# Where layer 0's sixth modulation vector is summed: inside the attention, or beside the attention's output projection

## The chip, the cores and the metric

The program runs on one core of a Trainium2 chip. The metric is the device time of one execution in microseconds. Five engines work side by side, each through its own list of instructions in a fixed order: TensorE (PE; its weight loads are PEld), VectorE (DVE), ScalarE (ACT), GpSimd (POOL) and SyncE (SP, which here issues the DMA transfers). An instruction that must wait for another engine or for a transfer holds up everything behind it on its own engine.

## The reference

A trunk of two layers over a sequence of 1024 rows of width 1024, all in float32. Layer 0 mixes by an attention with forget gates (16 heads of 64), layer 1 by gated linear attention (GLA), and each is followed by a SwiGLU channel mixer (FFN). Before and after each of these stand factors that are computed from one conditioning vector c:

```python
c_act = jax.nn.silu(c)
for i in range(DEPTH):
    mod = c_act @ ada_w[i] + ada_b[i]
    sh1, sc1, g1, sh2, sc2, g2 = jnp.split(mod, N_MOD, axis=-1)
    h = modulate(rms_norm(x, norm1_g[i]), sh1, sc1)
    ...
    x = x + g1[:, None, :] * y
    h = modulate(rms_norm(x, norm2_g[i]), sh2, sc2)
    x = x + g2[:, None, :] * swiglu(h, ffn_w_in[i], ffn_w_out[i])
```

So `mod` has six parts of 1024 numbers per layer, each a vector of 1024 times a matrix of 1024 x 1024. The kernel calls them j = 0 to 5. Layer 0's parts 0 and 1 are needed at the start, part 2 (the gate of the attention) from its output projection on, parts 3 and 4 when the channel mixer's input is made, and part 5 (the gate of the channel mixer) only where the channel mixer's output is added to x.

## The kernel before

Every large product is done as three products of rounded halves (`mm3`, L286 to L288: high by high, low by high, high by low), so each float32 operand is split into a high part (ScalarE, a cast) and a low part (VectorE or GpSimd, a subtraction). The attention of layer 0 goes over eight pairs of heads p = 0 to 7. While pair p's scores (L1132 to L1135), softmax (L1138 to L1144, VectorE, ScalarE and GpSimd), transposes (`t_b`, L1164) and outputs (L1176, L1178) are done, the projections of pair p + 1 are woven in between them on TensorE (`qk_proj`, `v_half`). The last pair, attention(7), is woven together with `fox_tail`: the output projection over the first four of eight blocks of the inner dimension (`out_chunk(0, 4, ...)`, tiles fo000 to fo071: block row m, half of the sequence). After it, `last_chunk(4, 4, ...)` does the other four blocks (tiles fo0400 and up for the first half, fo1401 and up for the second). Each group of products ends with a VectorE instruction that multiplies by the gate g1 and adds into x (L1277; in the changed file L1279). Sums of squares (`ss`, L718 and L725) for the next normalisation follow in `last_chunk`.

The modulation vectors are summed on VectorE by the generator `ada_steps(l, j, acc, raw_of, nt, ahead)`. One step loads nt x 128 rows of ada_w's part j by four DMAs (L423, each into 32 partitions) into a raw tile, and then does nt multiply-adds of 128 x 256 into the accumulator `acc` (L442 for the first of a vector, L444 for the others; c's numbers are the scalars). With nt = 4 a vector has 8 steps, with nt = 2 it has 16; either way it has 32 multiply-adds. At its end two small products with `four` (L449) add up the quarters, and VectorE adds ada_b (L452).

When a step is emitted is set by the class `Pace`: a call `ada0(t)` adds t to a balance, and steps are run as long as the balance is not negative, each taking off what it yields (1.0 for a step with ahead = 0). Before the change four vectors, j = 2 to 5, stand in the queue `ada0` as 8 steps and one end each, 36 units; `qk_proj` adds 3.3 at its end for p = 2 to 7, twice each, 12 times. Their raw tiles come from the ring `wr` of three slots, which the weight loads (L209) use as well. The accumulator `acc0` uses a quarter of a slot of its own, [128, 2, 512] float32: its first half's first 256 columns. Layer 1's vectors stand in a second queue, `ada1`, with nt = 2 and tiles named ad_s.

The emitted order is not yet the order on the engines. A scheduler with a timeline of its own orders each engine's instructions; `tc.issue_after(x)` adds the condition that an instruction comes behind x, and `last_of("D")` is the last instruction emitted for VectorE so far.

Of the kernel before, what the change touches and what calls it, by code (L numbers as in the profile page):

```python
# [9 lines left out]
F32 = mybir.dt.float32  # L10
# [6 lines left out]
P = 128  # L17
# [3 lines left out]
HALF = 512  # L21
# [32 lines left out]
def trunk(ctx, tc, x, c, ada_w, ada_b, norm1_g, norm2_g, ffn_w_in, ffn_w_out,  # L54
# [253 lines left out]
    acc_r = Ring(big, acc_sl)  # L308
# [65 lines left out]
    for t in range(6):  # L374
        nt, src = (4, rows2[0:8, :]) if t < 4 else (2, crow)
# [35 lines left out]
    def ada_steps(l, j, acc, raw_of, nt, ahead):  # L411


        steps, got = deque(range(32 // nt)), deque()

        def load():
            if not steps:
                return
            n = steps.popleft()
            raw = raw_of([P, nt * 256], F32, f"ada{l}{j}{n}").rearrange("p (t c) -> p t c", t=nt)  # L420
            src = ada_w[l, 32 * nt * n:32 * nt * (n + 1), j * D:(j + 1) * D]
            for q in range(4):
                nc.sync.dma_start(raw[32 * q:32 * q + 32],  # L423
                                  src[:, 256 * q:256 * q + 256].rearrange("(r t) c -> r t c", t=nt))
            got.append(raw)

        for _ in range(ahead):
            load()
        for n in range(32 // nt):
            load()  # L430
            if ahead:
                yield ADA_A
            raw = got.popleft()
            with ExitStack() as es:
                if ahead:
                    es.enter_context(tc.issue_after(last_of("D")))
                elif n == 0:
                    es.enter_context(tc.issue_after(split_after["D"]))
                for t in range(nt):
                    o = (0 if nt == 4 else 32) + t * (32 // nt) + n  # L440
                    if n == t == 0:
                        nc.vector.tensor_scalar(acc, raw[:, t], c42[:, o:o + 1], None, op0=ALU.mult)  # L442
                    else:
                        nc.vector.scalar_tensor_tensor(acc, raw[:, t], c42[:, o:o + 1], acc,  # L444
                                                       op0=ALU.mult, op1=ALU.add)
            yield ADA_B if ahead else 1.0
        mp = pj([P, 2, 4], F32, f"mp{l}{j}")
        for b in range(2):
            nc.tensor.matmul(mp[:, b], acc[:, psl(b)], four, start=True, stop=True)  # L449
        o = l * 48 + j * 8  # L450
        qb = lambda t: t.rearrange("p (q b) -> p b q", b=2)
        nc.vector.tensor_add(qb(modc[:, l, j]), mp, qb(vec[:, o:o + 8]))  # L452
        for i, jj in ((0, 1), (1, 4)):
            if j == jj:
                make_a(l, i)
        yield 1.0
# [23 lines left out]
    ada0, ada1 = Pace(), Pace()  # L480
# [616 lines left out]
    def qk_proj(p, i):  # L1097

        if i == 0:
            qkt[p] = qk_tiles(p)  # L1100
        wt = feed.next()
        feed.depth = 3
        for hf in range(2):
            ps = pj([P, HALF], F32, f"qk{i}{p}{hf}")
            yield from proj(ps, wt, hT, hf)
            (k_evac if i else q_evac)(ps, qkt[p], hf)
        if p > 1:
            ada0(3.3)

    oTs = {}  # L1110

# [95 lines left out]
    def attention(p):  # L1207
        for a in range(2):
            for g in ORDER:
                u = (p, a, g)  # L1210
                lps = yield from scores(u)
                if pending[0] is not None:
                    yield from finish(*pending[0])
                pending[0] = (u, lps)
        if p == 7:
            yield from finish(*pending[0])
# [2 lines left out]
        for g in gs:  # L1219
            yield from g  # L1220

    acc0 = acc_r([P, 2, HALF], F32, "acc0")[:, 0, 0:256]
    for j in (2, 3, 4, 5):
        ada0.q.append(ada_steps(0, j, acc0, wr, 4, 0))
    run(v_half(0, 0, gates_end))
    q_evac(accs[1][1][1], qkt[0], 1)
# [76 lines left out]
    oh = new_h("oh")  # L1303
    x_slots = idle + [list(otr.q)[-1]]
    xs = [big.tile([P, S], F32, tag=x_slots[k], name=f"x0_{k}") for k in range(8)]

    def fox_tail():
        for k in range(4):
            reload_h(oT_d, oh, k, "or")

        nc.sync.dma_start(xs[0], xT_d[0])

        def ahead(k):
            if 3 <= k < 6:
                reload_h(oT_d, oh, k + 1, "or")
            if k < 7:
                nc.sync.dma_start(xs[k + 1], xT_d[k + 1])
            yield 0.01

        yield from out_chunk(0, 4, oh, xs, 0, 2, "fo", (0, 1), before=ahead)  # L1320

    weave(attention(7), 27.0, fox_tail(), 36.0, LAGS)
    split(oh[7].hi, oh[7].lo, oTs[7])
    dump_d("oT", oT_d)
# [17 lines left out]
    def ffn(l, oh, xs, slots, nm, mid, norm_end, each=None):  # L1342
# [13 lines left out]
        pj, psr = ps_rings(6, 2)  # L1356
# [7 lines left out]
        sv = Views(slots["to"], 2, [HALF], f"ss{l}").v  # L1364
# [30 lines left out]
                split_t((b["B11"] + b["B21"])[k], ya[k], sh(k))  # L1395
            return gates

        last_chunk(4, 4, oh, xs, l, 2, nm, sv, norm, psr=psr)
        dump(f"xa{l}", xs)
        sg = opr_["sg"]  # L1400
        rb = rms_rows(ss1[0], f"{l}11", psr)
# [336 lines left out]
        sv = Views(slots["b"][0:4], 2, [HALF], f"se{l}").v  # L1738
# [27 lines left out]
    ADA_A, ADA_B = 6.0, 3.0  # L1766
# [25 lines left out]
    ADA_A, ADA_B = 2.6, 1.0  # L1792
# [260 lines left out]
    oh = new_h("gh")  # L2053
# [8 lines left out]
    xs = [big.tile([P, S], F32, tag=x_slots[k], name=f"x1_{k}") for k in range(8)]  # L2062
# [39 lines left out]
    ADA_A, ADA_B = 12.0, 6.0  # L2102
# [31 lines left out]
```

## Time and profile before

| | |
|---|---|
| median of 3 runs | 2396.82 us (2395.17 to 2397.31) |
| profiled execution | 2397.77 us |
| its span in the trace | 2396.1 us |
| granted TensorE clock | 0.997 |
| TensorE busy | 2368.3 us (99%) |
| VectorE busy | 1776.6 us (74%) |
| multiply-adds of layer 0's j = 2 to 5 | 142 to 474 us |
| first and last residual add of `fox_tail` | 522 and 601 us |
| residual adds of `last_chunk`, first half | 617 to 628 us |

The span is what the profiler saw from first to last instruction; the profiled execution's own time is 1.7 us longer. In the rows that are quoted below a line such as "L444 DVE" is the source line and the engine, an arrow leads from inputs to the output, and x is a count. A row of waits says which engine, at which line, waited for what: us in all, times, longest. A row of the chain has its start, its length and what it was. A row of the timeline has the start, the length, the instruction and, in brackets, how long the engine stood idle before it and what ended that.

### The profile page before, as it was taken

What the parts mean: (1) busy time and instruction counts of PE and PEld (TensorE: products, weight loads), DVE (VectorE), ACT (ScalarE), POOL (GpSimd) and SP (SyncE); (2) the same over time, 40 slices, a digit from 0 to 9 for tenths busy, and PEclk for the clock granted to TensorE, in tenths of its full rate; (3) what the DMA queues carried; (4) which work ended last, traced back from release to release, by engine and by line L of the source; (5) the groups of instructions that cost most, each with busy time, mean ns of one, the idle gap of its engine ahead of it and who ended that gap; (6) DMA issues with size and microseconds to landing.
All of it is one profiled execution on the core that took longest, in us unless ns stands there. A gap on an engine that the chain in (4) does not pass through costs nothing.

```text
span 2396.1 us, 35784 instructions
## 1 busy us (share of the span) xinstructions
PE 2368.3 (99%) x12344; PEld 2016.8 (84%) x12344; DVE 1776.6 (74%) x3016; ACT 1127.8 (47%) x2164; POOL 1008.5 (42%) x911
## 2 busy tenths in 40 slices
PE   8999999999999999999999999999999999999998
PEld 7888888888888888888888888898888888888888
DVE  6577878886698788876798666655687877775787
ACT  6666555674443333345325645353343333345326
POOL 1333333333445666643264321222345666643262
PEclk9999999999999999999999999999999999999999
DMA  7422424342435544557655242334424544457664
GB/s 254 145 89 90 131 84 128 106 138 83 150 109 173 179 166 165 171 196 261 229 187 162 67 119 80 107 112 135 136 96 161 183 145 159 154 182 256 228 202 146
DMA packets 335773, 363.42 MB, mean 152 GB/s; under 512 B 24348, under 2 KB 277432, under 8 KB 335592
## 3 DMA queue, kind: packets, MB, share of 16 engines
q1 hardware_dynamic: 335592, 361.15, 45.9%
q8 instruction: 97, 1.59, 0.3%
q14 instruction: 84, 0.69, 0.1%
HBM read 268.19 MB, written 92.86 MB: 151 GB/s over the span
## 4 chain that ended last, share of the span: by engine, by line
PE 90%; DVE 5%; DMA 2%; ACT 1%; issue 1%; POOL 0%; SPq 0%; DVEq 0%; POOLq 0%; ACTq 0%
PE p_b L288 16%; PE p_b L286 16%; PE p_b L287 16%; PE t_b L1164 2%; PE o_b L1178 2%; PE qk_b L286 2%; PE qk_b L287 2%; PE qk_b L288 2%; PE vps_b L286 1%; PE vps_b L288 1%; PE vps_b L287 1%; PE s_b L1132 1%; PE s_b L1133 1%; PE gr_b L286 1%; PE gr_b L287 1%
## 5 line engine op out<-in xcount | busy, mean ns | idle before, releaser
L175 DVE TENSOR_TENSOR o_s<-xv_s,o_s 128x512 fp32r<-128x512 f32 (+1 forms) x376 | 324.1, 867 | 66.1 <-ACT o_s L174 65.6
L174 ACT CAST o_s<-xv_s 128x512 fp32r<-128x512 f32 (+1 forms) x376 | 216.2, 587 | 303.6 <-PE p_b L288 248.0
L287 PE MATMUL p_b<-B,o_s 128*128 128x512 f32 x608 | 237.8, 391 | 0.0
L288 PE MATMUL p_b<-B,o_s 128*128 128x512 f32 x608 | 237.5, 391 | 0.0
L286 PE MATMUL p_b<-B,o_s 128*128 128x512 f32 x608 | 236.3, 392 | 0.0
L1144 POOL TENSOR_SCALAR lp_s<-lp_s,st 128x128 f32<-128x128 f32 (+7 forms) x128 | 99.0, 778 | 291.1 <-DVE st L1143 280.7
L843 POOL TENSOR_TENSOR ex_s<-xv_s,xv_s 128x512 f32<-128x512 f32 (+1 forms) x64 | 85.5, 1335 | 292.8 <-DMA xv_s<-in_ffn_w_in_dram 120.7
L286 PE MATMUL p_b<-T,o_s 128*128 128x512 f32 x480 | 186.7, 389 | 0.0
L287 PE MATMUL p_b<-T,o_s 128*128 128x512 f32 x480 | 186.7, 389 | 0.0
L288 PE MATMUL p_b<-T,o_s 128*128 128x512 f32 x480 | 181.2, 389 | 0.0
L287 PEld LDWEIGHTS p_b<-B,o_s 128*128 128x128 f32 x608 | 115.0, 189 | 23.9
L286 PEld LDWEIGHTS p_b<-B,o_s 128*128 128x128 f32 x608 | 115.0, 189 | 23.8
L288 PEld LDWEIGHTS p_b<-B,o_s 128*128 128x128 f32 x608 | 114.7, 189 | 24.0
L1142 ACT ACTIVATE lp_s<-lp_s,st 128x128 f32<-128x128 f32 (+7 forms) x128 | 99.3, 777 | 65.2 <-DVE st L1138 62.1
L174 ACT CAST pt_s<-t_b 128x512 fp32r<-128x512 f32 (+1 forms) x160 | 79.7, 547 | 75.4 <-PE t_b L1164 73.9
L845 POOL TENSOR_TENSOR xv_s<-ex_s,xv_s 128x512 f32<-128x512 f32 (+1 forms) x64 | 88.1, 1377 | 60.7 <-DVE o_s L175 58.2
L1521 DVE TENSOR_TENSOR ex_s<-ex_s,p_b 128x512 f32<-128x512 f32 x140 | 93.7, 681 | 23.4 <-PE p_b L288 23.2
L227 POOL TENSOR_TENSOR w_l_s<-w__s,w_h_s 128x256 fp32r<-128x256 f32 x90 | 69.7, 803 | 94.7 <-ACT w_h_s L223 56.7
L175 DVE TENSOR_TENSOR pt_s<-t_b,pt_s 128x512 fp32r<-128x512 f32 (+1 forms) x160 | 96.2, 631 | 15.9 <-ACT pt_s L174 15.3
L287 PEld LDWEIGHTS p_b<-T,o_s 128*128 128x128 f32 x480 | 90.1, 188 | 18.7
L286 PEld LDWEIGHTS p_b<-T,o_s 128*128 128x128 f32 x480 | 90.1, 188 | 18.7
L288 PEld LDWEIGHTS p_b<-T,o_s 128*128 128x128 f32 x480 | 90.1, 188 | 18.6
(1954 smaller groups left out, 7392.9 us busy)
## 6 DMA issues: line engine op xcount, KB each, us to landing
xv_s<-in_ffn_w_in_dram SPq DMA_DIRECT2D x176, 256.0 KB, 3.3
hid_B<-x SPq DMA_DIRECT2D x70, 512.0 KB, 2.6
ad_s<-in_ada_w_dram SPq DMA_DIRECT2D x384, 64.0 KB, 2.4
hid_T<-x SPq DMA_DIRECT2D x36, 512.0 KB, 2.8
xv_s<-in_ffn_w_out_dram SPq DMA_DIRECT2D x96, 192.0 KB, 5.3
ada_s<-in_ada_w_dram SPq DMA_DIRECT2D x128, 128.0 KB, 2.8
xv_s<-in_ffn_w_out_dram SPq DMA_DIRECT2D x40, 256.0 KB, 2.9
T2o<-hid_T SPq DMA_DIRECT2D x18, 512.0 KB, 8.4
```

What stands on the lines that cost most here:

```text
L174: nc.scalar.copy(hi, src)
L175: nc.vector.tensor_sub(lo, src, hi.bitcast(F32))
L227: (nc.gpsimd if i < 3 else nc.vector).tensor_sub(lo[:, cs], rw[:, cs], hi[:, cs].bitcast(F32))
L286: nc.tensor.matmul(ps, ah, bh, start=start, stop=False)
L287: nc.tensor.matmul(ps, ah, bl, start=False, stop=False)
L288: nc.tensor.matmul(ps, al, bh, start=False, stop=stop)
L843: nc.gpsimd.tensor_add(s1, a21, a22)
L845: nc.gpsimd.tensor_sub(a11, s1, a11)
L1142: nc.scalar.activation(lp, lp, AF.Exp, bias=mcur, scale=-1.0, accum_out=st[:, qi, 2:3])
L1144: nc.gpsimd.tensor_scalar(lp, lp, st[:, qi, 3:4], 1.0, op0=ALU.mult, op1=ALU.mult)
L1164: nc.tensor.transpose(tp[:, i, :], lps[qi][:, psl(2 * b + jj)], ident)
L1521: nc.vector.tensor_add(d, d if src is None else dest(G, src), ps)
```

## The change

Vector j = 5 leaves the queue that the attention works off. It is put into `ada0` again just before attention(7) and `fox_tail` are woven, with nt = 2, and its raw tile is the other half of the accumulator's slot (`raw0`), a single one. So each of its 16 steps loads 4 x 64 KB where a step before loaded 4 x 128 KB, and no load can start before the two multiply-adds of the step ahead of it have read `raw0`. The steps are paid by 1.05 after each of the 16 groups of `out_chunk`; a step takes off 0.7 + 0.3. The conditions `if ahead` become `if nt == 2`, so that j = 5 yields between its load and its multiply-adds and has its multiply-adds behind the last emitted VectorE instruction; for layer 1's vectors, all nt = 2, nothing differs. The pace in `qk_proj` goes from 3.3 to 2.4 a call, for 27 units. What might be left is paid in `last_chunk`, and a `flush` stands behind it.

```diff
@@ ada_steps
-            if ahead:
+            if nt == 2:
                 yield ADA_A
             raw = got.popleft()
             with ExitStack() as es:
-                if ahead:
+                if nt == 2:
                     es.enter_context(tc.issue_after(last_of("D")))
...
-            yield ADA_B if ahead else 1.0
+            yield ADA_B if nt == 2 else 1.0
@@ qk_proj
         if p > 1:
-            ada0(3.3)
+            ada0(2.4)
@@ the queue
-    acc0 = acc_r([P, 2, HALF], F32, "acc0")[:, 0, 0:256]
-    for j in (2, 3, 4, 5):
+    acc0 = acc_r([P, 2, HALF], F32, "acc0")
+    raw0 = acc0[:, 1]
+    acc0 = acc0[:, 0, 0:256]
+    for j in (2, 3, 4):
         ada0.q.append(ada_steps(0, j, acc0, wr, 4, 0))
@@ fox_tail
-        yield from out_chunk(0, 4, oh, xs, 0, 2, "fo", (0, 1), before=ahead)
-
+        yield from out_chunk(0, 4, oh, xs, 0, 2, "fo", (0, 1), before=ahead, after=lambda m, hf: ada0(1.05))
+
+    ADA_A, ADA_B = 0.7, 0.3
+    ada0.q.append(ada_steps(0, 5, acc0, Cycle([raw0]), 2, 0))
     weave(attention(7), 27.0, fox_tail(), 36.0, LAGS)
@@ ffn
-        last_chunk(4, 4, oh, xs, l, 2, nm, sv, norm, psr=psr)
+        last_chunk(4, 4, oh, xs, l, 2, nm, sv, norm, psr=psr, meanwhile=lambda: ada0(1.0))
+        ada0.flush()
```

The engines' orders differ from attention(1) up to the start of `last_chunk`; from there to the end of the program they are the same. The numbers in tile names count tiles and differ between the files. At three places:

SyncE's transfers in the second half of the projection (wo: the projection's weights; xv: the channel mixer's). Before:

```order
L209 DMA wo_768_s_78_7081<-in_fox_w_out_dram 128x4x256
L209 DMA wo_512_s_77_7040<-in_fox_w_out_dram 128x4x256
L209 DMA wo_0_s_79_7123<-in_fox_w_out_dram 128x4x256
L209 DMA wo_256_s_80_7164<-in_fox_w_out_dram 128x4x256
L825 DMA xv_s_7330<-in_ffn_w_in_dram 128x4x128 x2
L209 DMA wo_512_s_81_7244<-in_fox_w_out_dram 128x4x256
L209 DMA wo_768_s_82_7285<-in_fox_w_out_dram 128x4x256
```

And now (acc_s is the accumulator's slot, here its half `raw0`; x16 are four steps):

```order
L423 DMA acc_s_1_753<-in_ada_w_dram 32x2x256 x4
L209 DMA wo_768_s_70_7105<-in_fox_w_out_dram 128x4x256
L423 DMA acc_s_1_753<-in_ada_w_dram 32x2x256 x4
L209 DMA wo_512_s_69_7064<-in_fox_w_out_dram 128x4x256
L423 DMA acc_s_1_753<-in_ada_w_dram 32x2x256 x16
L209 DMA wo_0_s_71_7147<-in_fox_w_out_dram 128x4x256
L423 DMA acc_s_1_753<-in_ada_w_dram 32x2x256 x12
L209 DMA wo_256_s_72_7188<-in_fox_w_out_dram 128x4x256
L423 DMA acc_s_1_753<-in_ada_w_dram 32x2x256 x4
L825 DMA xv_s_7354<-in_ffn_w_in_dram 128x4x128 x2
L423 DMA acc_s_1_753<-in_ada_w_dram 32x2x256 x4
L209 DMA wo_512_s_73_7268<-in_fox_w_out_dram 128x4x256
```

The loads of steps 5 to 15 stand among the weight loads, four to sixteen at a time, and the weights and the channel mixer's first loads behind them.

VectorE's instructions from the last groups of `fox_tail` to the first residual add of `last_chunk` (lp, st and pt: softmax and the probabilities' low parts; oT: the attention's output; ohl: its low part). Before:

```order
L1277 SCALAR_TENSOR_TENSOR x_7_6234<-fo070p_b_63_6981,modc,x_7_6234 128x512
L1143 RECIPROCAL st_6858<-st_6858 128x1
L1193 TENSOR_TENSOR oT_s_8_6384<-o_b_63_6905,ot_6940 64x256
L1277 SCALAR_TENSOR_TENSOR x_7_6234<-fo071p_b_64_7006,modc,x_7_6234 128x512
L227 TENSOR_TENSOR wo_512l_s_66_7043<-wo_512_s_77_7040,wo_512h_s_65_7042 128x256
L175 TENSOR_TENSOR pt_s_158_6949<-t_b_158_6944,pt_s_158_6949 128x512
L175 TENSOR_TENSOR pt_s_159_6960<-t_b_159_6955,pt_s_159_6960 128x512
L175 TENSOR_TENSOR pt_s_160_6970<-t_b_160_6966,pt_s_160_6970 128x384
L227 TENSOR_TENSOR wo_256l_s_72_7167<-wo_256_s_80_7164,wo_256h_s_71_7166 128x256
L1193 TENSOR_TENSOR oT_s_8_6384<-o_b_64_6943,ot_6999 64x256
L175 TENSOR_TENSOR ohl_6226<-oT_s_8_6384,ohh_6225 128x1024
L1277 SCALAR_TENSOR_TENSOR x_0_6227<-fo0400p_b_1_7050,modc,x_0_6227 128x512
```

And now:

```order
L227 TENSOR_TENSOR wo_512l_s_66_7067<-wo_512_s_69_7064,wo_512h_s_65_7066 128x256
L1193 TENSOR_TENSOR oT_s_8_6324<-o_b_63_6905,ot_6946 64x256
L175 TENSOR_TENSOR pt_s_158_6955<-t_b_158_6950,pt_s_158_6955 128x512
L175 TENSOR_TENSOR pt_s_159_6966<-t_b_159_6961,pt_s_159_6966 128x512
L175 TENSOR_TENSOR pt_s_160_6976<-t_b_160_6972,pt_s_160_6976 128x384
L444 SCALAR_TENSOR_TENSOR acc_s_1_753<-acc_s_1_753,c_164 128x256 x2
L227 TENSOR_TENSOR wo_256l_s_72_7191<-wo_256_s_72_7188,wo_256h_s_71_7190 128x256
L1193 TENSOR_TENSOR oT_s_8_6324<-o_b_64_6949,ot_7013 64x256
L444 SCALAR_TENSOR_TENSOR acc_s_1_753<-acc_s_1_753,c_164 128x256 x2
L175 TENSOR_TENSOR ohl_6150<-oT_s_8_6324,ohh_6149 128x1024
L444 SCALAR_TENSOR_TENSOR acc_s_1_753<-acc_s_1_753,c_164 128x256 x2
L1279 SCALAR_TENSOR_TENSOR x_0_6151<-fo0400p_b_1_7074,modc,x_0_6151 128x512
```

The multiply-adds of steps 13, 14 and 15 stand between the attention's last instructions, step 15's right ahead of fo0400's residual add (step 12's stand two rows ahead of the first row here).

TensorE at the change from the fifth and sixth block rows of `last_chunk` to the seventh. Before:

```order
L287 MATMUL fo0440p_b_5_7133<-ohl_6226,wo_512h_s_65_7042 128x512
L288 MATMUL fo0440p_b_5_7133<-ohh_6225,wo_512l_s_66_7043 128x512
L287 MATMUL fo0450p_b_6_7148<-ohl_6226,wo_512h_s_65_7042 128x512
L288 MATMUL fo0450p_b_6_7148<-ohh_6225,wo_512l_s_66_7043 128x512
L286 MATMUL fo0460p_b_7_7174<-ohh_6219,wo_768h_s_67_7083 128x512
L287 MATMUL fo0460p_b_7_7174<-ohl_6220,wo_768h_s_67_7083 128x512
```

And now:

```order
L286 MATMUL fo0450p_b_6_7172<-ohh_6149,wo_512h_s_65_7066 128x512
L287 MATMUL fo0450p_b_6_7172<-ohl_6150,wo_512h_s_65_7066 128x512
L288 MATMUL fo0450p_b_6_7172<-ohh_6149,wo_512l_s_66_7067 128x512
L449 MATMUL mp_b_64_7040<-four,acc_s_1_753 128x4 x2
L286 MATMUL fo0460p_b_7_7198<-ohh_6143,wo_768h_s_67_7107 128x512
L287 MATMUL fo0460p_b_7_7198<-ohl_6144,wo_768h_s_67_7107 128x512
```

The two small products of vector 5, which need its finished sum, stand ahead of fo0460 now; the three products of fo0450 above them stood some rows further up before.

## The prediction

> **What bounds the kernel now.** I read the page's engine table first, then its chain, and after that, for the two stretches that the change touches, the windows, the waits and the chain inside them.
>
> ```profile
> span 2396.1 us, 35784 instructions
> PE 2368.3 (99%) x12344; PEld 2016.8 (84%) x12344; DVE 1776.6 (74%) x3016; ACT 1127.8 (47%) x2164; POOL 1008.5 (42%) x911
> PE 90%; DVE 5%; DMA 2%; ACT 1%; issue 1%; POOL 0%; SPq 0%; DVEq 0%; POOLq 0%; ACTq 0%
> ```
>
> TensorE bounds the program: 2368.3 of 2396.1 us busy, 90% of the chain. The change takes no product away, so time can come only out of the 27.8 us in which TensorE is idle, and be lost only by adding to them. Which of them lie in layer 0's attention, where steps are taken away, and which in the output projection, where they are put?
>
> ```profile
> 225.00:250.00 25.00, 23.72 (x170) 21.10 (x170) 21.17 (x56) 15.15 (x34) 8.64 (x11) 1.00 0.33 104
> 250.00:300.00 50.00, 48.79 (x310) 42.89 (x309) 39.98 (x107) 29.93 (x65) 18.03 (x26) 1.00 0.39 118
> 300.00:350.00 50.00, 50.00 (x334) 44.63 (x333) 36.96 (x91) 29.52 (x63) 20.07 (x28) 1.00 0.23 75
> 350.00:400.00 50.00, 47.92 (x335) 42.77 (x334) 41.59 (x112) 29.96 (x65) 18.82 (x26) 1.00 0.45 138
> 400.00:450.00 50.00, 49.41 (x339) 43.87 (x339) 40.43 (x103) 31.25 (x67) 17.80 (x25) 1.00 0.31 95
> 450.00:500.00 50.00, 48.68 (x289) 40.71 (x288) 40.34 (x109) 31.64 (x69) 18.42 (x24) 1.00 0.47 148
> 519.00:617.00 98.00, 97.46 (x563) 82.66 (x562) 63.73 (x158) 49.64 (x105) 31.86 (x40) 1.00 0.26 87
> 640.00:650.00 10.00, 10.00 (x50) 8.42 (x49) 10.00 (x17) 5.99 (x10) 0.00 (x0) 1.00 0.44 157
> ```
>
> The columns after the stretch are its length, then TensorE, its weight loads, VectorE, ScalarE and GpSimd. In 225 to 500, where the vectors j = 2 to 5 are summed, TensorE is idle 1.28 + 1.21 + 0 + 2.08 + 0.59 + 1.32 = 6.48 us (2.4%), and VectorE is busy 220.47 of 275 (80%). In 519 to 617, the projection, TensorE is idle 0.54 us (0.55%) and VectorE busy 63.73 of 98 (65%). Right behind it, in 640 to 650, VectorE is never idle.
>
> In the attention, who waits for whom:
>
> ```profile
> DVE acc_s L444 <- DMA ada_s<-in_ada_w_dram: 10.2, 8, 2.1
> SPq L423 <- DVE w_l_s L227: 39.8, 8, 8.9
> PE s_b L1132 <- DVE st L1138: 1.8, 3, 1.2
> PE t_b L1164 <- POOL lp_s L1144: 1.7, 1, 1.7
> ```
>
> VectorE stands 8 times, 10.2 us, before a multiply-add whose block of ada_w has not landed; SyncE's loads of it wait for ring slots that weight splits hold. The two longest TensorE waits:
>
> ```profile
> 292.78 0.33 PE L1132 MATMUL s_b<-KA,QA 128*128 128x128 f32 x1 [1.21 <-DVE st L1138]
> 356.24 0.55 PE L1164 MATMUL t_b<-ident,lp_s 128*128 128x128 f32 x3 [1.70 <-POOL lp_s L1144]
> ```
>
> The chain into the first of them shows one whole step of the vector sum:
>
> ```profile
> 264.14 0.56 SPq L423
> 264.74 0.60 SPq L423
> 265.39 0.60 SPq L423
> 266.03 2.77 DMA ada_s<-in_ada_w_dram
> 268.97 0.49 DVE acc_s L444
> ```
>
> The fourth of four transfers starts 266.03 − 264.14 = 1.89 us after the first, lands 2.77 later, and the multiply-add begins 0.17 after that. The chain into the other:
>
> ```profile
> 348.69 0.50 DVE acc_s L444
> 349.19 0.06 SPq L423
> 350.57 2.86 DMA ada_s<-in_ada_w_dram
> 353.52 0.49 DVE acc_s L444
> ```
>
> Here the slot is freed by a multiply-add that ends at 349.19, and the next one starts at 353.52: from slot to use 4.3 us. That is the shape of every step after the change, in which only one slot is left.
>
> **The change part by part.**
>
> Durations for both ends: the multiply-add, the small product at a vector's end, and the landing of 64 KB loads (ad_s, layer 1's vectors, later in the program) and of 128 KB loads:
>
> ```profile
> L444 DVE SCALAR_TENSOR_TENSOR acc_s<-ada_s,c,acc_s x124: 460/485/1227, 142.5 to 473.3; 128x256 f32<-128x256 f32 x124
> ad_s<-in_ada_w_dram SPq DMA_DIRECT2D x384, 64.0 KB, 2.4
> ada_s<-in_ada_w_dram SPq DMA_DIRECT2D x128, 128.0 KB, 2.8
> ```
>
> *Attention, a quarter of the steps gone.* Vector j = 5 is 32 multiply-adds, 32 × 0.485 = 15.5 us of VectorE, and 32 transfers on SyncE. VectorE falls from 220.47 to about 205 of 275, 80% to 74.5%. The trace has two points of idle TensorE against VectorE's load, 0.55% at 65% and 2.36% at 80%; a line between them gives 1.70% at 74.5%, so (2.36 − 1.70)% × 275 = 1.8 us less. The other reading is by cause: 1.2 + 1.7 = 2.9 us of TensorE waits end a chain with an ada_w transfer in it, and all of these go if the remaining steps are no longer late. I take the middle, **−2.3**. The ends: −6.5 (all idle time goes) and about +6.5 (the order of every row there is made anew, and the idle time could double). The three vectors left keep their way of summing. Where a stall goes, the next thing late is VectorE's softmax work itself, which the waits name already (L1138).
>
> *Projection, the steps added.* The same 15.5 us on VectorE, 64 transfers of 64 KB instead of 32 of 128 KB (same bytes, 32 more issues). VectorE goes from 63.73 to 79.2 of 98, 81%, where the attention showed 2.4% idle: up to 2.3 − 0.54 = 1.8 us. But the operations stand there in gaps (34 us of them), so I take half, **+0.9**, ends 0 and 1.8. The cover is this idle VectorE; without it the whole 15.5 us would go through.
>
> *The chain of the single slot.* Every load waits for the multiply-adds of the step before. The store on which step 4's last transfer stands behind on SyncE, and the softmax row beside its multiply-adds:
>
> ```profile
> 548.86 0.32 SPq L1205 DMA_DIRECT2D oT_d<-oT_s  x1
> 557.42 46.05 SPq L209 DMA_DIRECT2D wo_s<-in_fox_w_out_dram  x4
> ```
> ```profile
> 551.10 0.69 DVE L1138 CUSTOM_DVE_ANT_0 lp_s<-s_b,cum_s 128x512 f32<-128x512 f32 x1 [0.46 <-PE s_b L1135]
> 616.76 0.75 DVE L1277 SCALAR_TENSOR_TENSOR x<-fo0400p_b,modc,x 128x512 f32<-128x512 f32 x1 [4.80 <-PE fo0400p_b L288]
> 622.34 1.81 DVE L725 TENSOR_TENSOR ss_s<-ss_s 128x512 f32<-128x512 f32 x1 [0.58 <-ACT ss_s L718]
> 624.96 0.62 DVE L227 TENSOR_TENSOR wo_512l_s<-wo_s,wo_512h_s 128x256 fp32r<-128x256 f32 x1 [0.81 <-ACT wo_512h_s L223]
> ```
> ```profile
> 616.10 0.39 PE L287 MATMUL fo0400p_b<-ohl,wo_0h_s 128*128 128x512 f32 x1
> 618.82 0.39 PE L286 MATMUL fo0460p_b<-ohh,wo_768h_s 128*128 128x512 f32 x1
> 622.45 0.39 PE L286 MATMUL fo1401p_b<-ohh,wo_0h_s 128*128 128x512 f32 x1
> ```
>
> The fourth transfer of step 4 issues behind the store, at about 549.2, lands 2.4 later, and with two multiply-adds and one softmax row of 0.69 between them the step ends near 554 (an estimate from these rows). Each of the 11 steps after it costs 1.89 to the fourth issue + 2.4 landing + 0.14 (0.17 and 0.1 in the two chains) + 2 × 0.485 = 5.4 us, together 59.4. Between the two halves of five steps stand other operations, a row of 0.69 three times, and twice a row, a residual add of 0.75 and a shorter operation, about 1.6 us: 5.3 us in all (an estimate). Step 15 ends near 554 + 59.4 + 5.3 = 618.7. Step 14 then ends at 613.3, and the low part ohl behind it near 614.5, ahead of the product at 616.10 that needs it. Two things are behind step 15. On VectorE the residual add of fo0400, at 616.76 before, then starts 1.9 us late. On TensorE the two small products with `four` stand ahead of fo0460, which began at 618.82: they need the sum at 618.7, so they come just in time (0.25 us each, moved from the attention, at no cost). From fo0400 on, VectorE has 0.58 + 0.81 = 1.4 us of idle time up to 632, and none in 640 to 650, so of the 1.9 between 0.5 and 1.9 reaches TensorE. I take **+1.2**. SyncE's queue: the weights of the projection and two FFN loads now stand behind transfers that wait for a slot, each by one step at most, 5.4 us; the last of the four weights issued from 557 on, at 603, is used by fo1401 at 622, so that costs nothing; without this lead it would be 5.4 us once.
>
> [...] The rows of 2.4 and 2.8 us, issued by SyncE, agree that half the bytes save little, and are used.
>
> *Sum.* The rest of the program keeps its order and is costed at nothing. Against the profiled execution, 2397.77 us (span 2396.1 and 1.7 around it): 2397.77 − 2.3 + 0.9 + 1.2 = 2397.6. The median of the runs, 2396.82, is 0.95 lower, so 2396.6: no change.
>
> **The rivals.** A change under 0.2%, 4.8 us, can't be told from none.
>
> *Slower: the slot's chain binds.* If a load takes 3.0 us to land, the chain is 11 × 0.6 = 6.6 us longer, step 15 ends at 625.3, and fo0400's add and the two products hold VectorE and TensorE by 8.5 us less at most 1.4. The tail's term is then 7.1 to 8.5 in place of 1.2: 2396.6 + 6.6 = 2403.2. It decides from a landing of about 2.9 on (11 × 0.48 = 5.3). For it: 2.8 is the median of the larger loads, the longest took 4.2, and a late step delays every one behind it. Against it: 64 KB loads show 2.4, and 519 to 617 has only 0.26 of the DMA engines busy. [...]
>
> ```profile
> DMA to landing us min/median/max: 2.5/2.8/4.2
> ```
>
> *Slower: the new order of the attention.* Every row from 142 us to 520 is arranged again. If that doubles the idle 6.5 us, 2396.82 + 6.5 + 2.1 = 2405.4. Against it: the same kinds of work, less of them.
>
> *Faster: the attention loses all its idle time.* VectorE at 74.5% would keep ahead of TensorE everywhere: −6.5 and a tail of 1.0, 2391.3. For it: the longest waits go back to ada_w transfers, and VectorE's own 10.2 us of waiting is there too. Against it: softmax rows behind TensorE and ScalarE remain, and a stall removed is often met by the next.
>
> *It does nothing that counts:* the steps are hidden in both places, within 1 us of 2396.8.
>
> **How the numbers follow.** The forecast, with the case that it does nothing, 0.39, its own range 2392 to 2401.6. The slot's chain 0.26, the new order 0.09, all idle time gone 0.26. Hence faster 0.26, same 0.39, slower 0.35. The lowest possible is 2396.82 − 6.5 = 2390.3; a range of 2391 to 2405 leaves out about half of the new order's cases, the chain with landings over 3.2 us, and the floor itself, some 0.2 together.
>
> **What would show it.** In 225 to 500 idle TensorE near 4.2 us, and less than 10.2 us of VectorE waits for ada_w. From 523 to 617 sixteen loads, one at a time, about 5.4 us from one to the next; VectorE near 79 of 98, TensorE idle under 1.5. Step 15 ending at 617 to 619 and fo0400's add right behind. Wrong if landings in the tail are near 3 us, if VectorE's gaps don't lie where the loads land, so that softmax rows stand behind waiting multiply-adds (the wait is in order, and TensorE's scores hang on them), or if the new order of the attention stalls elsewhere.

## The result and the profile after

| | before | after |
|---|---|---|
| median of 7 runs | 2397.22 us (2395.17 to 2400.98) | 2404.32 us (2403.66 to 2406.66) |
| profiled execution, its span | 2397.77, 2396.1 us | 2406.66, 2405.0 us |

The changed kernel is slower: the ratio is 1.0031 (95% interval 1.0019 to 1.0043), 7 us on the medians, 8.9 us between the two profiled executions (that of the changed kernel is the slowest of its seven runs). That is inside the range of the prediction and outside its likeliest case. The engine table and the chain by engine, after:

```profile
PE 2371.8 (99%) x12344; PEld 2016.0 (84%) x12344; DVE 1780.7 (74%) x3016; ACT 1128.1 (47%) x2164; POOL 1007.3 (42%) x911
PE 82%; DVE 7%; DMA 5%; issue 2%; ACT 2%; SPq 1%; POOL 1%; DVEq 0%; POOLq 0%; ACTq 0%
```

TensorE has the same products and is busy 3.5 us longer (2368.3 before). Its share of the chain fell from 90 to 82%; transfers (5% instead of 2%) and VectorE (7% instead of 5%) took most of that. The two stretches of the prediction, after:

```profile
225.00:500.00 275.00, 271.41 (x1789) 239.17 (x1788) 212.40 (x547) 170.29 (x368) 100.98 (x140) 1.00 0.32 100
519.00:617.00 98.00, 94.82 (x533) 78.30 (x533) 73.86 (x179) 46.67 (x99) 28.85 (x37) 1.00 0.37 116
```

In the attention TensorE is idle 3.6 us instead of 6.5, in the projection 3.2 instead of 0.5. To see where time is won and lost, I follow the same products through both programs. TensorE's timeline, before:

```profile
514.26 0.40 PE L286 MATMUL fo000p_b<-ohh,wo_0h_s 128*128 128x512 f32 x1
612.70 0.39 PE L286 MATMUL fo0450p_b<-ohh,wo_512h_s 128*128 128x512 f32 x1
1319.17 0.50 PE L286 MATMUL gr_b<-h1h,w_h_s 128*128 128x512 f32 x1 [0.39 <-DVE gvt_s L175]
```

And after:

```profile
510.68 0.39 PE L286 MATMUL fo000p_b<-ohh,wo_0h_s 128*128 128x512 f32 x1
614.64 0.39 PE L286 MATMUL fo0450p_b<-ohh,wo_512h_s 128*128 128x512 f32 x1
622.26 0.61 PE L449 MATMUL mp_b<-four,acc_s 128*128 128x4 f32 x4 [0.99 <-DVE acc_s L444]
623.01 0.47 PE L286 MATMUL fo0460p_b<-ohh,wo_768h_s 128*128 128x512 f32 x1
1325.73 0.50 PE L286 MATMUL gr_b<-h1h,w_h_s 128*128 128x512 f32 x1 [2.19 <-DVE gvt_s L175]
```

- The first product of the projection starts 3.6 us earlier: the attention's gain.
- fo0450 starts 1.9 us later: the projection lost 5.5 us between the two. TensorE has the same products between these places in both programs.
- fo0460 starts 4.2 us later (618.82 before): another 2.3 lost at the two small products.
- The offset is 4.4 to 4.5 us through the whole channel mixer, up to about 1250.
- At gr, the first gate product of layer 1's GLA, TensorE waits 2.19 instead of 0.39 us, and the offset is 8 us behind it. It is 8.9 at the end.

So a stage that the prediction held to be untouched lost 3.5 us. I had compared the orders of the engines too coarsely: the text on the change says that nothing differs behind the start of `last_chunk`, and that is wrong. At the start of the GLA a few rows stand elsewhere. ScalarE's and VectorE's halves of one split (gvt, the low and high parts of a value tile) come one to two rows later. VectorE's rows there (h1l: the low parts of the normalised rows), before:

```order
L687 SCALAR_TENSOR_TENSOR h1l_12609<-te_s_12430,modc,h1h_12608 128x512
L175 TENSOR_TENSOR gvt_s_2_13036<-gv_b_2_12987,gvt_s_2_13036 128x512
L687 SCALAR_TENSOR_TENSOR h1l_12613<-te_s_12431,modc,h1h_12612 128x512
```

And after:

```order
L687 SCALAR_TENSOR_TENSOR h1l_12633<-te_s_12454,modc,h1h_12632 128x512
L687 SCALAR_TENSOR_TENSOR h1l_12637<-te_s_12455,modc,h1h_12636 128x512
L175 TENSOR_TENSOR gvt_s_2_13060<-gv_b_2_13011,gvt_s_2_13060 128x512
```

The split of gvt, which TensorE's gr waits for, now stands behind the last normalised row. The scheduler works along one timeline, and steps that were moved 700 us earlier in the program tipped a decision here.

The chain through the end of the projection, after (start, length, what):

```profile
615.89 0.50 DVE acc_s L444
616.41 0.57 SPq L423
618.29 2.25 DMA acc_s<-in_ada_w_dram
620.76 0.94 DVE acc_s L444
621.72 0.48 DVE acc_s L444
622.20 0.67 DVE x L1279
```

This is the single slot's chain in the form that the prediction described: the load starts when the multiply-adds end (616.39 to 616.41), its fourth part starts 1.88 us later, lands in 2.25, and the sum ends at 622.20, with fo0400's residual add right behind it.

### The profile page after: what moved, and what is told of

Its sections match the earlier page's. It is cut to its first block, busy times and chain, and to the rows that moved or that the text cites. A ratio compares the mean times of both kernels' runs of the same rounds, so it can differ in the third digit from the quotient of the medians.

```text
span 2405.0 us, 35818 instructions
## 1 busy us (share of the span) xinstructions
PE 2371.8 (99%) x12344; PEld 2016.0 (84%) x12344; DVE 1780.7 (74%) x3016; ACT 1128.1 (47%) x2164; POOL 1007.3 (42%) x911
## 4 chain that ended last, share of the span: by engine, by line
PE 82%; DVE 7%; DMA 5%; issue 2%; ACT 2%; SPq 1%; POOL 1%; DVEq 0%; POOLq 0%; ACTq 0%
PE p_b L288 15%; PE p_b L286 15%; PE p_b L287 15%; PE o_b L1178 2%; PE t_b L1164 2%; PE qk_b L286 2%; PE qk_b L287 2%; PE qk_b L288 2%; PE vps_b L288 1%; PE vps_b L286 1%; PE vps_b L287 1%; DMA acc_s<-in_ada_w_dram 1%; PE gr_b L286 1%; PE gr_b L287 1%; PE s_b L1132 1%
```

## The experiments

All times are medians; each difference is to the kernel before in runs on the same chip (its medians there: 2398.91 for the first four, 2398.20 for the next four, 2398.25 for the three after them and 2398.65 for the last). The ratio in brackets, with its 95% interval, goes by all runs and not by the medians, so the two can differ by a microsecond or two. My theory after the two traces: the attention gains 3.6 us; the projection loses 5.5 among the attention's rows and 2.3 at the end of the sum, because of the single slot; the order of the GLA's start loses 3.5.

### Without the vector

```diff
-    ada0.q.append(ada_steps(0, 5, acc0, Cycle([raw0]), 2, 0))
+    nc.vector.tensor_copy(modc[:, 0, 5], vec[:, 40:48])
```

> The changed kernel without vector j = 5: its 16 steps and its two small products are left out, and the channel mixer's gate is ada_b alone, copied into place. The pace of 2.4 in the attention stays, and so does the order of the rest of the program as it was before the change. Theory (the attention gained 3.6 us, and all that is lost lies behind it): about 2393.5 us, 3.6 below before, with TensorE in the projection as little idle as before (0.5 us). Rival (the new order of the attention gives nothing, and the earlier start of the projection in the changed kernel's trace is that execution's luck): 2397.

2394.95 us, 4.0 below (ratio 0.9988, 0.9979 to 0.9997). The projection, by windows:

```profile
519.00:617.00 98.00, 97.68 (x562) 83.00 (x562) 64.54 (x157) 50.93 (x108) 32.33 (x42) 1.00 0.25 84
```

TensorE is idle 0.3 us there. The gain of a lighter attention is real, 3 to 4 us, and everything else that the change does costs 10 to 11. The size is not sharper than that: the interval goes from 0.7 to 5.0 us, and in this trace fo0460 starts 2.3 us earlier (616.50); the other 1.6 us come in 640 to 740, where this execution lacks a stretch at half the clock that the kernel before has (0.83 granted in 655 to 665, 1.00 here).

### The steps without their loads

In `load`, steps of the projection take the tile as it is; it is filled once ahead of them:

```diff
+            if nt == 2 and l == 0:
+                steps.popleft()
+                got.append(raw_of().rearrange("p (t c) -> p t c", t=nt))
+                return
...
+    nc.vector.memset(raw0, 0.001)
```

> The changed kernel, whose 16 steps in the projection load nothing: the raw tile is filled once with a constant, so the multiply-adds of j = 5 run on that, and all 32 of them stand where they stood. The start of the GLA keeps the changed kernel's order. Theory (the loss in the projection is the single slot's round of issue, landing and use, with attention work queued behind it): 2397.2 - 3.6 (attention) + 1.5 (VectorE's extra work) + 3.5 (order of the GLA) = about 2398.6 us; TensorE in 519 to 617 idle 1 to 2 us. Rival (VectorE's 15.5 us of extra work is the loss, whatever it waits for): as slow as the changed kernel, 2404.

2402.36 us, 3.5 above (1.0016, 1.0006 to 1.0026). In its trace fo000, fo0450 and fo0460 start at:

```profile
510.66 0.40 PE L286 MATMUL fo000p_b<-ohh,wo_0h_s 128*128 128x512 f32 x1
612.49 0.39 PE L286 MATMUL fo0450p_b<-ohh,wo_512h_s 128*128 128x512 f32 x1
618.61 0.39 PE L286 MATMUL fo0460p_b<-ohh,wo_768h_s 128*128 128x512 f32 x1
```

Against the kernel before, −3.6, −0.2, −0.2. So without any load the projection still loses 3.4 of its 5.5 us, where I had expected 1 to 2, and nothing at the end of the sum. The rival, that VectorE's work is all of it, is refuted too: it lies between. (This profiled execution, 2396.39 us, was the fastest of 11; the median says 3.5 above.) The longest wait of TensorE in this stretch does not stand directly behind a multiply-add:

```profile
552.28 1.06 ACT L174 CAST ohh<-or_s 128x1024 fp32r<-128x1024 f32 x1 [0.48 <-DMA or_s<-oT_d]
553.37 1.23 DVE L175 TENSOR_TENSOR ohl<-or_s,ohh 128x1024 fp32r<-128x1024 f32 x1 [1.38 <-ACT ohh L174]
555.25 0.62 PE L1182 MATMUL o_b<-pt_s,v_s 128*128 128x256 f32 x3 [0.87 <-DVE pt_s L175]
```

The split of a reloaded part of the attention's output (or_s) waits for its reload and stands ahead of the pt that TensorE needs; before the change this split's cast stands behind three casts of pt (553.62 and 555.06). So the 3.4 us are the added work together with the order that was made new around it; no run separates the two.

### The order of the GLA alone

On the kernel before, the split of that one tile is put behind the instructions h6 of the other half's normalisation:

```diff
-        split(v[:, 0], v[:, 1], ps)
+        with ExitStack() as es:
+            if h == 0 and tp == 1:
+                es.enter_context(tc.issue_after(h6["A"]))
+                es.enter_context(tc.issue_after(h6["D"]))
+            split(v[:, 0], v[:, 1], ps)
```

> The kernel before, with one thing done: at the start of the GLA the split of the second value tile (gvt: ScalarE's cast and VectorE's subtraction) is put behind the fourth normalised row of the other half, as in the changed kernel. The scheduler then also puts two small products of the gate (z) two places later; nothing else moves. Theory (this order makes TensorE wait for a PSUM bank that the split frees, 2.2 us at 1325 in the changed kernel, and 3.5 us in all): 2400.7 us. Rival (the stall there comes from the lower granted clock or a late weight load in that one execution): 2397.2, no change.

2401.41 us, 2.5 above (1.0012, 1.0003 to 1.0020). Its gr product, and the windows around it of this kernel:

```profile
1321.57 0.50 PE L286 MATMUL gr_b<-h1h,w_h_s 128*128 128x512 f32 x1 [2.32 <-DVE gvt_s L175]
```
```profile
1310.00:1320.00 10.00, 9.25 (x64) 8.26 (x62) 8.33 (x13) 7.12 (x12) 3.18 (x4) 1.00 0.48 102
1320.00:1330.00 10.00, 8.43 (x34) 6.96 (x35) 3.28 (x4) 3.66 (x7) 2.88 (x3) 0.83 0.00 0
```

The one swap makes the wait (0.39 to 2.32 us), and in the ten microseconds of the wait the granted clock is 0.83 on average, 1.7 us of TensorE time. Before the change these windows read:

```profile
1310.00:1320.00 10.00, 9.61 (x63) 8.48 (x63) 8.74 (x13) 7.72 (x13) 3.29 (x4) 1.00 0.45 87
1320.00:1330.00 10.00, 10.00 (x65) 9.08 (x64) 3.37 (x4) 3.76 (x7) 2.82 (x3) 1.00 0.01 2
```

1.9 of wait and 1.7 of clock are the 3.5 us between the two traces.

### One transfer for a step

```diff
+            if nt == 2 and l == 0:
+                nc.sync.dma_start(raw, src.rearrange("(r t) (q c) -> q r t c", t=nt, q=4))
+            else:
```

> The changed kernel with each of the 16 loads in the projection as one transfer of 256 KB instead of four of 64 KB. One raw tile still, and the same multiply-adds; the scheduler orders the start of the GLA as before the change. Theory (the chain of the single slot binds, and 1.9 us of each step of 5.9 are the four issues): 0.6 to issue + about 3 to land + 1.1 = 4.7 us a step, below the 5.3 us in which TensorE goes through a group, so the chain hides: 2397.2 - 3.6 + 1 to 2 = about 2395 us. Rival (VectorE's work is the loss): 2404.3 - 3.5 for the order of the GLA = 2400.8.

2442.13 us, 43 above (1.0182): a miss of 47 us, and on neither side. (The expectation is also wrong on the GLA: its order there is the changed kernel's, with a wait of 2.2 us.) Two of its landings in the projection, and what VectorE and TensorE wait for most from 505 to 640:

```profile
558.58 7.47 DMA acc_s<-in_ada_w_dram
575.51 5.80 DMA acc_s<-in_ada_w_dram
DVE acc_s L447 <- DMA acc_s<-in_ada_w_dram: 38.7, 13, 5.6
PE s_b L1135 <- DVE st L1141: 11.0, 4, 4.1
PE o_b L1181 <- ACT pt_s L174: 7.8, 2, 7.1
```

From issue to landing, six of these 256 KB transfers from 550 to 596 took 5.8 to 7.5 us, where I had taken about 3 from others of the same size in the page before (xv_s, medians 3.3 and 2.9). That page also has 256 KB transfers with a median of 6.4: adas_s, from ada_w too. Why this form lands late is not shown. What the miss does show: from step 1's issue to step 15's a step takes 8.1 us (521.60 to 634.49), in the changed kernel 6.8 (520.98 to 616.41). The last load is issued 18 us later than there, but fo0460 starts 37 us later (660.02). So it is not the end of the sum that costs most: softmax rows stand behind multiply-adds whose block has not landed, and TensorE waits for these rows.

### Two tiles instead of one

The steps are done in halves of 256 columns, and the next half is loaded while one is used (32 half steps, 128 transfers of 32 KB):

```diff
-    ada0.q.append(ada_steps(0, 5, acc0, Cycle([raw0]), 2, 0))
+    ada0.q.append(half_steps(0, 5, acc0, [raw0[:, 0:256], raw0[:, 256:512]]))
```

> The changed kernel, whose raw tile is used as two tiles of 256 columns: each step is done in two halves, each with its own four transfers (of 32 KB) and one multiply-add, and the next half is loaded while one is used. Memory, multiply-adds and place stay; the transfers double to 128. The start of the GLA keeps the changed kernel's order. Theory (the round of load and use with one tile costs 4.4 of the 8.0 us lost in the projection, the rest is VectorE's extra work between the attention's): the last multiply-add is done before fo0400's residual add, TensorE has no wait before the two small products, and the time is 3 to 4 us above the kernel before, like the kernel without loads. Rival (the number of transfers on SyncE, 0.6 us each, sets the pace of the chain): 32 x 2.4 = 77 us still fit, but with the other loads between them they don't; as slow as the changed kernel, 7 above, or slower.

2400.91 us, 2.7 above (1.0013, 1.0005 to 1.0022), about as the theory had it. TensorE's waits from 505 to 660 in this kernel:

```profile
PE o_b L1210 <- DVE pt_s L175: 2.3, 3, 0.9
PE s_b L1164 <- DVE st L1170: 1.1, 1, 1.1
```

The wait at the two small products is gone; these waits of the attention's last rows for VectorE's pt and st stay (fo0450 starts at 614.50 and fo0460 at 620.62, both 1.8 later than before the change).

### The ring of three slots

```diff
-    ada0.q.append(ada_steps(0, 5, acc0, Cycle([raw0]), 2, 0))
+    ada0.q.append(ada_steps(0, 5, acc0, wr, 4, 0))
```

with `ada0(0.56)` after each group instead of 1.05.

> The changed kernel, with j = 5 in the projection as 8 steps of four multiply-adds, loaded by four transfers of 128 KB into the ring of three slots that the projection's weights use too, paced 0.56 a group. Theory (waiting for the single tile is what the projection loses): 3 to 4 us above the kernel before, as two tiles do. Rival (the ring's slots are the scarce thing, and weights and reloads of the attention's output come late): TensorE waits for weights (L223 and L227 behind L209), 7 us above or more.

2405.44 us, 7.2 above (1.0031, 1.0019 to 1.0042). The time is the rival's; its reason is seen in part. TensorE's longest waits there, none of them for weights:

```profile
PE s_b L1132 <- DVE st L1138: 1.8, 2, 1.0
PE o_b L1178 <- DVE pt_s L175: 1.5, 2, 0.9
PE fo010p_b L286 <- DVE x L1279: 1.2, 1, 1.2
```

A fourth, 1.2 us for ScalarE's pt, and 0.9 of the waits for VectorE's pt (at 559 and 560) stand behind the split of a reloaded or_s, as in the kernel without loads, and ScalarE waited 0.4 us for that reload. The two waits for st stand where multiply-adds lie between the softmax rows (five from 533.4 to 540.4). The clock adds to it: 0.98 granted over 519 to 617, 1.00 before the change. More slots alone don't help.

### In the channel mixer

Vector 5 is put behind layer 1's vectors 0 and 1 in the second queue, which is paid 0.96 x n instead of 0.64 x n.

> Vector j = 5 is summed neither in the attention nor in the projection, but in layer 0's channel mixer, behind layer 1's vectors 0 and 1 in the second queue, with that queue's three tiles; the queue is paid 0.96 instead of 0.64 there, the attention keeps 2.4. The start of the GLA is ordered as before the change. Theory (the attention gains 3 us, and VectorE, 66 to 82% busy in the channel mixer at no idle TensorE, hides 15.5 us): 3 us below the kernel before, as without the vector. Rival (VectorE or SyncE is late for the mixer's products, where every add follows a product): 0 to 5 us above.

2415.91 us, 17.7 above (1.0074, 1.0060 to 1.0088). TensorE's waits in 650 to 1100, of which there were none before:

```profile
PE p_b L286 <- DVE x L1523: 7.1, 8, 1.5
PE p_b L286 <- DVE sg_s L1523: 3.9, 6, 1.5
```

VectorE 66 to 83% busy over 100 us looked like room. But each product here hands its PSUM bank to a VectorE add (L1523), and multiply-adds at a higher pace stand in front of these. The gain before 620 was there (fo000 2.8 us earlier); the mixer lost 17 between 650 and 1080, beyond the 0 to 5 of the rival too. That the adds are late because of the multiply-adds ahead of them is the plainest reading of these waits; no run tests it alone.

### The end of the sum put later

```diff
+        if l == 0 and nt == 2:
+            yield 100.0
         mp = pj([P, 2, 4], F32, f"mp{l}{j}")
```

> The changed kernel, but the end of vector j = 5 (two small products and the add of ada_b) is emitted behind the last group of the projection instead of ahead of fo0460. Loads, steps and the GLA's order stay. Theory (the two products hold TensorE there until the sum is done, 2.3 us): about 2 us below the changed kernel, 5 above the one before. Rival (fo0400's residual add, which waits behind step 15 on VectorE, holds the PSUM banks just as long): no difference to the changed kernel, 7 above.

2405.83 us, 7.6 above (1.0024, 1.0014 to 1.0035). The interval, 3.4 to 8.4 us, holds the theory's 5 and the rival's 7, so the time does not decide; the trace does, and for the rival. TensorE waits at the same place for something else:

```profile
PE fo0460p_b L286 <- DVE x L1281: 1.8, 1, 1.8
```

That is fo0400's residual add, which stands behind step 15 on VectorE and frees the bank that fo0460 writes. The two small products only happened to wait there too.

### The changed kernel with the GLA in its old order

`ada0(2.2)` instead of 2.4 in the attention is enough to tip the scheduler back.

> The changed kernel with 2.2 instead of 2.4 a call in the attention, so that the last fraction of vectors 2 to 4 is paid at its end. The scheduler then orders the start of the GLA as before the change; the attention and the projection are arranged a little differently, with the same steps in them. Theory (the order of the GLA's start costs 3.5 us, a stall and a stretch at half clock behind it): between 1250 and 1375 no time is lost against the kernel before, and the whole is 3 to 4 us above it instead of 7. Rival (every arrangement with the vector in the projection loses there too): the stall of about 2 us before gr stays, 7 above.

2402.73 us, 4.5 above (1.0022, 1.0013 to 1.0032), against 7 for the changed kernel; the interval, 3.1 to 7.7 us, does not shut out the rival, so the trace has to decide. TensorE's only wait in 1300 to 1340:

```profile
PE gr_b L286 <- DVE gvt_s L175: 0.8, 1, 0.8
```

Between 1250 and 1375 the offset to the kernel before grows by 0.5 us instead of 3.5. So the loss there is gone with the swap, as the theory had it. The projection itself is no better in this kernel (fo0460 at 625.13).

### Begun earlier, in the kernel before

The calls after the projections of p = 1 pay too, in the first kernel 6.0 with 2.0 for the others:

```diff
-        if p > 1:
-            ada0(3.3)
+        if p > 0:
+            ada0(2.0 if p > 1 else 6.0)
```

> The kernel before, with the four vectors begun earlier: the calls after the projections of p = 1 pay too, 6.0 each, and the others 2.0 instead of 3.3 (12 + 24 = 36 units). Nothing is moved into the projection; the start of the GLA keeps the order of the kernel before. Between 100 and 200 us VectorE was 57 to 80% busy with TensorE idle 0.7 us. Theory (VectorE's load from 225 on makes the attention's idle TensorE, and an earlier stretch takes the steps for nothing): 2 to 4 us below the kernel before. Rival (the ring's slots are short there, since the loads of the weights for v and q wait behind it): TensorE stalls before 225, no gain or slower.

2411.16 us, 12.9 above (1.0052, 1.0040 to 1.0065). The stretch from 75 to 225, in which TensorE was idle 0.7 us before:

```profile
75.00:225.00 150.00, 139.81 (x918) 123.63 (x918) 110.30 (x265) 82.02 (x165) 50.79 (x69) 0.99 0.39 117
```

It is idle 10.2 us now, and 7.8 of these are waits for VectorE's pt, st and oT. The rival has the outcome; of its reason, late weights, 1.3 us of waits are seen.

The milder form pays 3.0 for p = 1 and 2.5 for the others:

> As the last, with 3.0 for p = 1 and 2.5 for the others, so that fewer steps are early (6 + 30 = 36 units); the start of the GLA is ordered as in the kernel before. Theory: 1 to 2 us below the kernel before, about half of the gain. Rival: no gain, as the stalls of the attention come from places and not from load.

2398.27 us, no difference (1.0001, 0.9992 to 1.0010). Idle TensorE moved from 225 to 500 (3.9 us left) to 75 to 225 (1.8 instead of 0.7) and elsewhere; nothing is won.

### By other engines

In the two-tile form, ScalarE scales a half step in its tile, and GpSimd adds it to the sum:

```diff
-            with tc.issue_after(last_of("D")):
-                ... (VectorE's multiply-add)
+            with tc.issue_after(last_of("A")):
+                nc.scalar.activation(raw, raw, AF.Identity, scale=c42[:, o:o + 1])
+            with tc.issue_after(last_of("G")):
+                nc.gpsimd.tensor_tensor(acc, acc, raw, op=ALU.add)
```

> The two-tile form of the changed kernel, with vector j = 5 summed by other engines: ScalarE scales each half of a step in its tile, GpSimd adds it to the sum; VectorE does none of it. The attention keeps 2.4, and the start of the GLA is ordered as in the kernel before. Theory (in the projection VectorE's extra work between the attention's rows makes TensorE wait 3.4 us even without loads, so without it only the attention's gain is left): 1 to 3 us below the kernel before. Rival (ScalarE's casts and GpSimd's scaling of the probabilities stand on the same path of the softmax, and their operations on 128 x 256 are longer): TensorE waits for pt and lp, 3 to 8 us above the kernel before.

2403.30 us, 4.6 above (1.0017, 1.0008 to 1.0026): the rival. VectorE is as little busy in the projection as before the change (61.5 of 98 us, 63.7 before); an operation on 128 x 256 takes ScalarE 0.51 and GpSimd 0.74 us (medians), where VectorE's multiply-add takes 0.485, and TensorE waits for ScalarE instead (1.3 us more for its pt):

```profile
PE fo0460p_b L286 <- ACT wo_768h_s L223: 2.1, 1, 2.1
```

No kernel here with the whole vector in it beats the one before.

## Why the prediction was wrong

It said no change, 2396.6 us; the time is 2404.32. Its steps, against the two traces:

- **Attention, −2.3 forecast: −3.6 measured** (−4.0 on the medians without the vector). The reason held in the main: of the two waits behind ada_w transfers the first, 1.2 us at 293, is gone, and so is one of 1.2 at 239 for VectorE's QB. The second, 1.7 us for lp, is gone at 356, but one as long before the same line came at 416, and its chain has an ada_w transfer in it too.
- **VectorE's extra work in the projection, +0.9 forecast: +5.5 measured** up to fo0450. This term was mis-sized most. I had priced the busy share by a line between two stages and halved it, because the operations lie in gaps. That left out what stands behind an operation in VectorE's fixed order, and that the order of the other rows is made new as well: 3.4 us are lost even if no step waits for data (the kernel without loads). How much of these 3.4 us is the one and how much the other stays open. The rest, by difference 2.1, goes with steps that wait for their block while softmax rows stand behind them:

```profile
DVE acc_s L444 <- DMA acc_s<-in_ada_w_dram: 15.4, 10, 3.2
```

  At 592, for one, VectorE's pt starts at 592.17, right behind a multiply-add that stood 2.84 us before its block; ScalarE's cast for it had ended by 588.48, and TensorE waits 0.68 us for this pt.

- **The chain of the single slot, +1.2 forecast: +2.3 measured.** The mechanism was right, its length was not: step 15 ended at 622.20, not 618.7. SyncE's rows show the round:

```profile
566.37 21.50 SPq L423 DMA_DIRECT2D acc_s<-in_ada_w_dram  x16
616.41 2.48 SPq L423 DMA_DIRECT2D acc_s<-in_ada_w_dram  x4
```

  From step 7's first issue to step 15's are 8 rounds in 50.04 us, 6.26 each, everything between the halves included, against 5.4 and 5.3 / 11 = 5.9 in the forecast. Landings of 64 KB were as forecast near the end (2.25 to 2.37), but one in these rounds took 4.27 us (from 587.28, with a weight load issued at 587.92), and several multiply-adds took 0.8 to 0.95 us instead of 0.485, the first of step 15 among them. And I let the lateness leak into VectorE's idle time; fo0460 needs the bank that fo0400's add frees (the kernel with the end put later shows this wait, 1.8 us), so VectorE's idle time behind that add took nothing off.
- **"The rest of the program keeps its order and is costed at nothing": +3.5 measured**, at the GLA's start. This step failed outright, and it is what takes the result from "4.4 slower" to over 0.2%. The same swap alone on the kernel before makes the same wait and the same loss of clock (2.5 us on the medians, interval 0.7 to 4.8), and the changed kernel with another pace, in which the swap doesn't occur, has a wait of 0.8. How much it costs hangs on the clock too (last section).
- What is left, about 0.9 us between 2190 and 2350 us of the profiled execution, wasn't followed up.

Of the rivals, "the slot's chain binds" (2403.2) and "the new order of the attention" (2405.4) both came within about 1.1 us, the second by luck: the attention's idle time fell instead of doubling. The first is right in part: the round was longer (6.26 us against 5.9), but the median landing was 2.4 us and not 3.0, and most of the loss was in the order around it. A sign that the prediction named did come: softmax rows stood behind waiting multiply-adds. It had no price in the sum.

## What to carry to other kernels

Work that is moved into idle time of an engine isn't free when that engine works in a fixed order (here the projection lost 5.5 us, with VectorE 75% busy): look at what stands behind each moved operation and who waits for it, and price that, not the busy share. One buffer makes each step pay issue, landing and use in a row (6.26 us a round here), and what stands behind the last step pays the sum of all delays (2.3 us here). Where a scheduler orders the whole program from one timeline, compare the orders to the very end before costing the rest at nothing: here two rows swapped 700 us away cost 3.5 of the 8.9 us between the two traces.

## What the runs showed of the hardware

*A wait can be followed by half the clock, and half the clock can hide a wait.* Three windows of 3.4 us in the changed kernel, 14 us ahead of gr's wait, with the wait in it, and right behind it (the granted clock is the third number from the end):

```profile
1309.30:1312.70 3.40, 3.40 (x18) 3.40 (x17) 1.38 (x3) 0.18 (x1) 3.38 (x4) 0.50 0.61 169
1323.00:1326.40 3.40, 1.22 (x6) 0.71 (x5) 1.83 (x2) 3.38 (x7) 2.14 (x3) 1.00 0.00 0
1326.40:1329.80 3.40, 3.40 (x10) 2.63 (x9) 1.36 (x2) 0.85 (x2) 1.71 (x2) 0.50 0.00 0
```

3.4 us at half the clock (0.50) cost 1.7. Seven traces with the swapped order have such a stretch some 15 us ahead of gr and waits of 1.7 to 2.3 us. Five of them show a second stretch right behind the wait (0.83 granted in ten microseconds there), and the kernel without loads, with the shortest wait, shows none (1.00 granted from 1320 to 1330).

Five traces with the old order and the first stretch have waits of 0.2 to 0.8 us and no second stretch (1.00 granted from 1315 to 1345). The last two with the old order (the vector in the channel mixer, and begun earlier) have no first stretch (1.00 granted from 1295 to 1345): TensorE comes earlier, waits 3.2 and 2.7 us for the same split, and keeps its clock. So the wait's length does not decide alone.

Where the wait falls may. In the traces before and after the change the stretches start whole multiples of 3.41 us apart (1309.3 and 1326.4 above are five apart). On that grid the wait of the changed kernel lies whole in one window, with 2.2 us of idle TensorE in it. So does that of the order alone, by an estimate: 0.87 granted in 1315 to 1325 and 0.96 in 1325 to 1335 put its second stretch at 1322.4, and its wait goes from 1319.25 to 1321.57. The wait of the vector in the channel mixer is spread over two windows:

```profile
1331.20:1334.60 3.40, 1.54 (x7) 0.94 (x5) 1.75 (x3) 3.40 (x7) 1.19 (x1) 1.00 0.00 0
1334.60:1338.00 3.40, 2.09 (x9) 1.75 (x10) 2.51 (x3) 3.38 (x8) 1.80 (x3) 1.00 0.00 0
```

Both of its windows are idle for 1.3 to 1.9 us. As a rule this is too loose: a wait of 1.8 us is followed by a stretch in the kernel with the ring (0.83 granted from 1325 to 1335), 1.9 us idle in a window here are not. And a stretch can come with no idle TensorE ahead of it: in the changed kernel TensorE is busy 3.40 of 3.40 us from 1305.9 to 1309.3, right before the first. What decides is not shown.

Most such stretches come at the same few places of the program (before the change near 65, 660, 1305, 1740 and 2395 us), but not in every execution: from 655 to 665 the kernel without the vector was granted 1.00, the one before 0.83. Two profiled executions can differ by one or two of them, 1.7 us each, that a change did not make; the medians here carry that spread (19 runs of the kernel before were granted 0.992 to 0.997).
